# Hymba layer on one core: loads of w_down columns by row block instead of by expert

## Chip, cores and metric

The kernel runs on one core of one Trainium2 chip. The metric is the device time of one execution in microseconds, as the median of several runs.

## What is computed

One layer of a decoder trunk for 256 tokens of width 2048 in float32: a combined projection with a convolution group and an attention group, an output projection, a mixture of experts (32 experts, two for each token), and a gated embedding branch. The change touches the last product of the experts and, through the order of loads, the gate product behind it:

```python
h = h + mixed @ w_out[i]
h = h + hierarchical_moe(rms_norm(h, norm_ffn[i]), ...)
gate = jax.nn.sigmoid(rms_norm(h, norm_ple[i]) @ w_ple_gate[i])
h = h + gate * (p[i] @ w_ple[i])

def expert_block(args):                     # for each expert e
    xb = xt[toks]                           # its tokens
    hidden = jax.nn.silu(xb @ w_gate[e]) * (xb @ w_up[e])
    y = hidden @ w_down[e]                  # w_down[e]: 512 x 2048
    return y * ws[:, None].astype(y.dtype)
```

All weights are float32 and each is read once, some 480 MB in all.

## The kernel before

**Waves.** The 32 experts are worked on in eight waves of four. In a wave each expert has up to 32 tokens, and the four experts share TensorE: expert e of the wave uses the column strip `tile_position=(0, 32 * e)`, so four matmuls of 32 columns run side by side. `gate_up` multiplies the tokens with w_gate and w_up, and its result is turned into `hTw(w)`: for each of four blocks j of 128 rows of w_down, the stationary operand of 32 columns per expert. Each float32 matmul of this kind shows as two records, called passes here.

**w_down.** For a wave, 512 output columns are 16 matmuls: for j in 0..3, for e in 0..3, all accumulating over j in one PSUM tile. For waves 0 to 3 (`NROW` is 4) `down_rows` does all four blocks of 512 columns straight after `gate_up`, from loads of whole rows (`want_rows`). For waves 4 to 7 `down_rows` does the first 1024 columns, from loads of half rows (`want_halves`); in wave 7 it runs all j of the first 512 columns and then all j of the second. The last 1024 columns of waves 4 to 7 come after all waves: `down_wave` runs for w = 4..7 with columns 1024 to 1535 (`TC[2]`) and then for w = 4..7 with columns 1536 to 2047 (`TC[3]`), eight calls in all, from loads that `want_d` lists. Between these calls stand steps of the gate product (`steps(1)`, 12 matmuls at lines 1176 to 1178) and `scatter` (line 1078), which adds a wave's result to the tokens.

**What follows a wave.** `outputs` lets ScalarE write `yh` (line 1071) and VectorE `yl` (line 1072) from the PSUM tile; `scatter` needs both. After the last call come an activation table load (line 1267), a cast and a subtraction of the next gate weight piece (`split`, lines 347 and 348, from a load of w_ple_gate), `add_down` (line 1123), the transposes of the last 512 columns, the last eight gate steps and the output (lines 1306 to 1309).

**Loads.** The order of all loads is a list that `want` fills. `pump` issues them from SyncE's queue (line 76) in this order as long as one of the 26 ring tiles of 1 MB (`NSLOT`) is free; `free(n)` gives back n tiles in program order and calls `pump`. A load whose tile was used before waits on SyncE for the last reader of that tile. Behind the half rows of wave 7 the list holds, in turns, four loads of `want_d` for one wave and, behind six of the eight waves, two loads of w_ple_gate, then two more of w_ple_gate at the very end.

The lines that the prediction follows:

```python
def want_d(w, c0, n):
    for e in range(4 * w, 4 * w + 4):
        want(("d", e, c0), [128, 4, n], w_down[e].rearrange("(j p) n -> p j n", p=128)[:, :, c0:c0 + n])
```

Of the kernel before, what the change touches and what calls it, by code (L numbers as in the profile page):

```python
# [25 lines left out]
NROW = 4  # L26
# [4 lines left out]
def kernel(ctx: ExitStack, tc: tile.TileContext, I, out):  # L31
    nc = tc.nc
    x, p = I["x"][0], I["p"][0, 0]
    w_in, w_out = I["w_in"][0], I["w_out"][0]
    w_gate, w_up, w_down = I["w_gate"][0], I["w_up"][0], I["w_down"][0]
# [18 lines left out]
    def alloc(shape, dt, name):  # L54
        used[0] += 1
        if name != "ld":
            KEEP[0] = max(KEEP[0] - 1, 0)
        assert used[0] <= NSLOT, (name, used, KEEP, nxt, loads[nxt[0]][0])
        return R.tile(shape, dt, name=name, tag="ring")

    loads, nxt, arrived = [], [0], {}

    def want(key, shape, src):
        loads.append((key, shape, src))

    def pump():
        while nxt[0] < len(loads) and used[0] < NSLOT - KEEP[0]:
            key, shape, src = loads[nxt[0]]
            nxt[0] += 1
            t = alloc(shape, F32, "ld") if shape else None  # L70
            i = 0
            for part in src if isinstance(src, list) else [src]:
                if callable(part):
                    part()
                    continue
                nc.sync.dma_start(t[:, i] if isinstance(src, list) else t, part)  # L76
                i += 1
            arrived[key] = t

    def free(n=1):  # L80
        used[0] -= n
        pump()

    def ps():
        return PS.tile([128, 512], F32, name="pst", tag="ps")

    def pa():
        return PA.tile([128, 2, 512], F32, name="pat", tag="pa")
# [47 lines left out]
                         wt[e].rearrange("(p j) f -> p j f", j=16)[:, 4 * j4:4 * j4 + 4, :])  # L136

    def want_d(w, c0, n):
        for e in range(4 * w, 4 * w + 4):
            want(("d", e, c0), [128, 4, n], w_down[e].rearrange("(j p) n -> p j n", p=128)[:, :, c0:c0 + n])  # L140

    def want_rows(w):
        for j in range(4):
# [1 line left out]
                want(("r", e, j), [128, D], w_down[e, 128 * j:128 * j + 128, :])  # L145

    def want_halves(w):
        for jp in range(2):
            for e in range(4 * w, 4 * w + 4):
                want(("r", e, jp), [128, 2, 1024],  # L150
                     w_down[e, 256 * jp:256 * jp + 256, 0:1024].rearrange("(j p) n -> p j n", p=128))

    TC = [(0, 512), (512, 512), (1024, 512), (1536, 512)]
    w_pg_v = w_pg.rearrange("(k p) n -> p k n", p=128)
# [21 lines left out]
    for (ci, w), nxt_ in zip(order, halves_):  # L176
        want_d(w, *TC[ci])
        if nxt_:
            want_pg(nxt_[0], 2 * nxt_[1], 2 * nxt_[1] + 1)
# [839 lines left out]
    def down_rows(w):  # L1019

        hv = hTw(w).rearrange("p (j s) -> p j s", j=4)
        nn = 4 if w < NROW else 2
        pts = [ps() for _ in range(nn)]

        def block(j, n):
            for e in range(4):
                if w < NROW:
                    d = arrived["r", 4 * w + e, j]
                else:
                    d = arrived["r", 4 * w + e, j // 2][:, j % 2]  # L1030
                nc.tensor.matmul(pts[n][32 * e:32 * e + 32, :], hv[:, j, 32 * e:32 * e + 32],  # L1031
                                 d[:, 512 * n:512 * n + 512], start=j == 0, stop=j == 3, tile_position=(0, 32 * e))

        def sums(n, y):
            ns = slice(512 * n, 512 * n + 512)
            po = pa()
            scatter(po, w, y, True, True)
            for tt in range(2):
                if w == 0:
                    if n == 0:  # L1040
                        macc[tt] = alloc([128, D], F32, "macc")
                    nc.vector.tensor_copy(macc[tt][:, ns], po[:, tt])
                else:
                    to = (hmid if w == NW - 1 else macc)[tt][:, ns]
                    nc.vector.tensor_add(to, po[:, tt], to)

        if w == NW - 1:
            for j in range(4):
                block(j, 0)
            y = outputs(pts[0], w)  # L1050
            for j in range(4):
                if j == 2:
                    sums(0, y)
                block(j, 1)
            free(8)
            y = outputs(pts[1], w)
            rows(0)
            sums(1, y)
            return
        for j in range(4):  # L1060
            for n in range(nn):
                block(j, n)
            if w < NROW or j % 2:
                free(4)
        for n in range(nn):
            sums(n, outputs(pts[n], w))

    def outputs(pt, w):

        yh, yl = (w2([128, 512], nm, F32R) for nm in ("yh", "yl"))  # L1070
        nc.scalar.activation(yh, pt, AF.Copy, scale=sw[:, w:w + 1])  # L1071
        nc.vector.scalar_tensor_tensor(yl, pt, sw[:, w:w + 1], yh.bitcast(F32), op0=OP.mult, op1=OP.subtract)  # L1072
        return yh, yl

    def scatter(po, w, y, start, stop):
        for tt in range(2):
            for i in range(2):
                nc.tensor.matmul(po[:, tt], sT(w)[:, 128 * tt:128 * tt + 128], y[i],  # L1078
                                 start=start and i == 0, stop=stop and i == 1)
# [29 lines left out]
    def down_wave(w, c0, cn):  # L1109

        pt = ps()
        hv = hTw(w).rearrange("p (j s) -> p j s", j=4)
        for j in range(4):
            for e in range(4):
                nc.tensor.matmul(pt[32 * e:32 * e + 32, :], hv[:, j, 32 * e:32 * e + 32],  # L1115
                                 arrived["d", 4 * w + e, c0][:, j, :],
                                 start=j == 0, stop=j == 3, tile_position=(0, 32 * e))
        free(4)
        return outputs(pt, w)

    def add_down(po, c0, cn):
# [20 lines left out]
    def rows(ci):  # L1142

        c0, cn = TC[ci]
        kn, k0 = cn // 128, c0 // 128
        hs = hsb[ci % 2]
        src = []
        for tt in range(2):
            src.append(ps().rearrange("p (k t) -> p k t", k=4))
            for kk in range(kn):  # L1150
                nc.tensor.transpose(src[tt][:, kk], acc[tt][:, c0 + 128 * kk:c0 + 128 * kk + 128], ident)
        for tt in range(2):
            tm = w2([128, 4, 128], "tm")
            nc.vector.tensor_tensor(tm, src[tt],
                                    g_ple[:, k0:k0 + kn, None].to_broadcast([128, kn, 128]), op=OP.mult)
            hh = hs[:, :, 128 * tt:128 * tt + 128]
            nc.scalar.copy(hh, tm)
            nc.vector.tensor_sub(hs[:, :, 256 + 128 * tt:384 + 128 * tt], tm, hh.bitcast(F32))
# [88 lines left out]
    for w in range(NROW, NW):  # L1247
        y = down_wave(w, *TC[2])
        steps(1)
        scatter(po, w, y, w == NROW, w == NW - 1)  # L1250
        if w < NW - 1:
            steps(1)
            if w == NROW:
                rows(1)
                squares(1)
            steps(1)
# [185 lines left out]
```

## Time and profile before

| | |
|---|---|
| median of 3 runs | 1362.25 us (1362.24 to 1362.37) |
| profiled execution, its own time | 1362.01 us |
| profiled execution, span of the trace | 1360.3 us |
| TensorE matmuls busy | 1137.8 us, 84% of the span |
| VectorE / ScalarE / GpSimd busy | 410.6 / 265.8 / 122.6 us |
| data moved | 484.29 MB, mean 356 GB/s |
| share of DMA in the chain that ended last | 48% |
| share of TensorE in it | 40% |

The times of the trace count from the start of its span. A busy share is a mean over stages with different limits, so it is read by stretch. Matmuls are pipelined: where one stands still for its data, the records before it are still running, and the idle time shown is shorter than the time lost. A share of DMA above 1 means that packets overlap on the engines.

### The profile page before, as it was taken

How to read it: one execution, taken by the hardware profiler on the slowest of the kernel's cores; microseconds unless marked ns; L12 is line 12 of the kernel's file. 1: busy time of each engine (PE TensorE's matmuls, PEld its weight loads, DVE VectorE, ACT ScalarE, POOL GpSimd, SP SyncE). 2: the span in 40 equal slices, each digit the busy share in tenths (PEclk: the TensorE clock that was granted, in tenths of full speed). 3: DMA queues.
4: the chain of work that ended last, by engine and by line, in shares of the span. 5: the costliest groups of instructions: out<-in, count | busy, mean ns of one | idle time of the engine just before them, and what ended most of it. 6: DMA issues, size and time to landing. Idle time of an engine off the chain costs nothing.

```text
span 1360.3 us, 14996 instructions
## 1 busy us (share of the span) xinstructions
PE 1137.8 (84%) x6171; PEld 633.3 (47%) x6172; DVE 410.6 (30%) x623; ACT 265.8 (20%) x435; POOL 122.6 (9%) x150
## 2 busy tenths in 40 slices
PE   8999899999998787668677775966986876689997
PEld 7888778888663251215125121511531511136655
DVE  6747877655411210201111020110110120124536
ACT  6435455544101000000000000000010000024324
POOL 2214577100000000000000000000000000000000
PEclk9999999999998888889879879998988988889999
DMA  8992245976899999999999999999999999999981
GB/s 261 311 343 80 77 154 175 376 240 221 345 421 420 421 421 421 421 422 420 422 421 421 422 421 422 414 420 421 414 420 421 415 420 422 414 396 394 392 339 63
DMA packets 133141, 484.29 MB, mean 356 GB/s; under 512 B 12020, under 2 KB 49292, under 8 KB 92876
## 3 DMA queue, kind: packets, MB, share of 16 engines
q1 hardware_dynamic: 131916, 480.37, 89.6%
q0 software_dynamic: 864, 2.40, 0.5%
q8 instruction: 50, 0.82, 0.2%
q10 hardware_dynamic: 288, 0.52, 0.2%
q14 instruction: 23, 0.19, 0.0%
HBM read 478.80 MB, written 4.19 MB: 355 GB/s over the span
## 4 chain that ended last, share of the span: by engine, by line
DMA 48%; PE 40%; DVE 5%; ACT 3%; issue 2%; SPq 1%; POOL 1%; ACTq 0%; DVEq 0%; POOLq 0%
DMA ld<-in_w_up_dram 33%; DMA ld<-in_w_down_dram 14%; PE pat L774 7%; PE pst L955 5%; PE pat L971 4%; PE pat L775 3%; PE pat L752 2%; PE pat L754 2%; PE pat L753 2%; PE pst L1115 2%; SPq L76 1%; PE pst L1098 1%; PE pst L1031 1%; DVE wsp L348 1%; PE pat L1078 1%
## 5 line engine op out<-in xcount | busy, mean ns | idle before, releaser
L971 PE MATMUL pat<-ld,xg 128*32 128x512 f32 x2048 | 328.2, 674 | 105.7 <-DMA ld<-in_w_up_dram 60.7
L971 PEld LDWEIGHTS pat<-ld,xg 128*32 128x32 f32 x2048 | 77.1, 121 | 345.9 <-issue 154.6
L774 PE MATMUL pat<-xs,wsp 128*128 128x512 f32 x544 | 197.1, 404 | 0.0
L1031 PE MATMUL pst<-ld,wv 128*32 128x512 f32 x768 | 151.9, 777 | 47.5 <-DMA ld<-in_w_down_dram 42.7
L775 PE MATMUL pat<-xs,wsp 128*128 128x256 f32 x544 | 154.0, 283 | 1.5 <-DVE wsp L348 1.5
L348 DVE TENSOR_TENSOR wsp<-ld,wsp 128x1024 fp32r<-128x1024 f32 x91 | 131.0, 1444 | 74.8 <-ACT wsp L347 74.8
L957 DVE TENSOR_TENSOR xg<-pst,gffn 128x512 f32<-128x512 f32 (+1 forms) x33 | 22.3, 676 | 400.1 <-PE pst L955 400.1
L347 ACT CAST wsp<-ld 128x1024 fp32r<-128x1024 f32 x104 | 107.9, 1048 | 87.2 <-PE pat L754 43.9
L955 PEld LDWEIGHTS pst<-sel,x 128*128 128x128 f32 x512 | 112.7, 311 | 8.4 <-issue 5.0
L774 PEld LDWEIGHTS pat<-xs,wsp 128*128 128x128 f32 x544 | 103.5, 190 | 27.8 <-issue 2.9
L955 PE MATMUL pst<-sel,x 128*128 128x128 f32 x512 | 114.8, 384 | 0.0
L1031 PEld LDWEIGHTS pst<-ld,wv 128*32 128x32 f32 x768 | 33.0, 135 | 160.4 <-DMA ld<-in_w_down_dram 80.8
L1008 ACT ACTIVATE sg<-pat 128x512 f32<-128x512 f32 x8 | 4.8, 597 | 523.3 <-PE pat L971 523.3
L775 PEld LDWEIGHTS pat<-xs,wsp 128*128 128x128 f32 x544 | 104.3, 192 | 2.4 <-DVE wsp L348 2.4
L1072 DVE SCALAR_TENSOR_TENSOR yl<-pst,sw,yh 128x512 fp32r<-128x512 f32 x32 | 23.9, 747 | 229.4 <-ACT yh L1071 229.4
L1071 ACT ACTIVATE yh<-pst,sw 128x512 fp32r<-128x512 f32 x32 | 22.0, 688 | 239.1 <-PE pst L1031 181.1
L948 POOL TENSOR_TENSOR sel<-sel,et 128x128 f32<-128x128 f32 x16 | 6.1, 400 | 643.2 <-DVE sel L946 643.2
L1078 PE MATMUL pat<-yl,wv 128*128 128x512 f32 x64 | 31.6, 493 | 27.4 <-DVE yl L1072 27.3
L752 PE MATMUL pat<-wsp,mx 128*128 128x512 f32 (+1 forms) x128 | 49.8, 389 | 0.1
L753 PE MATMUL pat<-wsp,mx 128*128 128x512 f32 (+1 forms) x128 | 49.0, 383 | 0.0
L754 PE MATMUL pat<-wsp,mx 128*128 128x512 f32 (+1 forms) x128 | 49.0, 383 | 0.0
L348 DVE TENSOR_TENSOR wsq<-ld,wsq 128x1024 fp32r<-128x1024 f32 x32 | 38.6, 1222 | 15.9 <-ACT wsq L347 15.9
(273 smaller groups left out, 1065.1 us busy)
## 6 DMA issues: line engine op xcount, KB each, us to landing
ld<-in_w_gate_dram SPq DMA_DIRECT2D x128, 1024.0 KB, 19.8
ld<-in_w_up_dram SPq DMA_DIRECT2D x128, 1024.0 KB, 11.1
ld<-in_w_down_dram SPq DMA_DIRECT2D x128, 1024.0 KB, 19.8
ld<-in_w_in_dram SPq DMA_DIRECT2D x35, 1024.0 KB, 13.1
ld<-in_w_out_dram SPq DMA_DIRECT2D x16, 1024.0 KB, 8.2
ld<-in_w_ple_gate_dram SPq DMA_DIRECT2D x16, 1024.0 KB, 17.1
spill<-x POOLq DMA_DIRECT2D x8, 256.0 KB, 4.8
ld<-in_w_ple_dram SPq DMA_DIRECT2D x2, 1024.0 KB
```

The source lines that it names most:

```text
L347: copy(t[:, :, 0], src)
L348: eng.tensor_sub(t[:, :, 1], src, t[:, :, 0].bitcast(F32))
L752: nc.tensor.matmul(o, mh, ws[:, kk, 0, cs], start=first, stop=False)
L753: nc.tensor.matmul(o, mh, ws[:, kk, 1, cs], start=False, stop=False)
L754: nc.tensor.matmul(o, ml, ws[:, kk, 0, cs], start=False, stop=last)
L774: nc.tensor.matmul(pt[:, b, :], ws[:, kk, 0, bs], xk, start=first, stop=False)
L775: nc.tensor.matmul(pt[:, b, 0:256], ws[:, kk, 1, bs], xk[:, 0:256], start=False, stop=last)
L955: nc.tensor.matmul(pt[:, 128 * jj:128 * jj + 128], hmid[tt][:, j::16], sel[w][:, tt], start=tt == 0, stop=tt == 1)
L971: nc.tensor.matmul(pt[32 * e:32 * e + 32, n, :], g[:, j, 32 * e:32 * e + 32], wt, start=j == 0, stop=j == 15, tile_position=(0, 32 * e))
L1031: nc.tensor.matmul(pts[n][32 * e:32 * e + 32, :], hv[:, j, 32 * e:32 * e + 32], d[:, 512 * n:512 * n + 512], start=j == 0, stop=j == 3, ti ...
L1078: nc.tensor.matmul(po[:, tt], sT(w)[:, 128 * tt:128 * tt + 128], y[i], start=start and i == 0, stop=stop and i == 1)
L1115: nc.tensor.matmul(pt[32 * e:32 * e + 32, :], hv[:, j, 32 * e:32 * e + 32], arrived["d", 4 * w + e, c0][:, j, :], start=j == 0, stop=j == ...
```

## The change

A load for `down_wave` still holds 512 columns in a tile of 128 partitions x 4 x 512. Before, the 4 are the row blocks j of one expert; after, they are the four experts of the wave, for one row block j. A load of half rows still is 128 x 2 x 1024. Before, the 2 are two neighbouring row blocks of one expert, and the loads of a wave come as experts 0 to 3 for blocks 0 and 1, then for blocks 2 and 3; after, the 2 are two neighbouring experts, for one row block, and the loads come block by block. The matmuls and their order stay. Tiles are given back after each block: one in `down_wave`, two in `down_rows` for half rows (wave 7 still gives back its eight at the end).

```diff
     def want_d(w, c0, n):
-        for e in range(4 * w, 4 * w + 4):
-            want(("d", e, c0), [128, 4, n], w_down[e].rearrange("(j p) n -> p j n", p=128)[:, :, c0:c0 + n])
+        for j in range(4):
+            want(("d", w, j, c0), [128, 4, n],
+                 w_down[4 * w:4 * w + 4, 128 * j:128 * j + 128, c0:c0 + n].rearrange("e p n -> p e n"))
...
     def want_halves(w):
-        for jp in range(2):
-            for e in range(4 * w, 4 * w + 4):
-                want(("r", e, jp), [128, 2, 1024],
-                     w_down[e, 256 * jp:256 * jp + 256, 0:1024].rearrange("(j p) n -> p j n", p=128))
+        for j in range(4):
+            for e in range(4 * w, 4 * w + 4, 2):
+                want(("r", e, j), [128, 2, 1024],
+                     w_down[e:e + 2, 128 * j:128 * j + 128, 0:1024].rearrange("e p n -> p e n"))
...
                 if w < NROW:
                     d = arrived["r", 4 * w + e, j]
                 else:
-                    d = arrived["r", 4 * w + e, j // 2][:, j % 2]
+                    d = arrived["r", 4 * w + e // 2 * 2, j][:, e % 2]
...
         for j in range(4):
             for n in range(nn):
                 block(j, n)
-            if w < NROW or j % 2:
-                free(4)
+            free(4 if w < NROW else 2)
...
         for j in range(4):
             for e in range(4):
                 nc.tensor.matmul(pt[32 * e:32 * e + 32, :], hv[:, j, 32 * e:32 * e + 32],
-                                 arrived["d", 4 * w + e, c0][:, j, :],
+                                 arrived["d", w, j, c0][:, e, :],
                                  start=j == 0, stop=j == 3, tile_position=(0, 32 * e))
-        free(4)
+            free()
         return outputs(pt, w)
```

The order of instructions on every engine stays; what moves is which of them wait for a load. On TensorE, the last call of `down_wave` (wave 7, columns 1536 on) before; `ld` is a load's tile, `wv` holds hTw, and DMAHW5, 6, 7 and 0 are the semaphores of its four loads in the order of issue:

```order
L1178 MATMUL pst<-wsq_5924,hs 128x512
L1115 MATMUL pst<-ld,wv 32x512 [waits DMAHW5_49]
L1115 MATMUL pst<-ld,wv 32x512 [waits DMAHW6_49]
L1115 MATMUL pst<-ld,wv 32x512 [waits DMAHW7_49]
L1115 MATMUL pst<-ld,wv 32x512 [waits DMAHW0_49]
L1115 MATMUL pst<-ld,wv 32x512 x12
```

and the same call after:

```order
L1178 MATMUL pst<-wsq_5924,hs 128x512
L1115 MATMUL pst<-ld,wv 32x512 [waits DMAHW5_49]
L1115 MATMUL pst<-ld,wv 32x512 x3
L1115 MATMUL pst<-ld,wv 32x512 [waits DMAHW6_49]
L1115 MATMUL pst<-ld,wv 32x512 x3
L1115 MATMUL pst<-ld,wv 32x512 [waits DMAHW7_49]
L1115 MATMUL pst<-ld,wv 32x512 x3
L1115 MATMUL pst<-ld,wv 32x512 [waits DMAHW0_49]
L1115 MATMUL pst<-ld,wv 32x512 x3
```

The wait for the fourth load has moved from the fourth of the 16 matmuls to the thirteenth.

On TensorE, the half rows of wave 7 in `down_rows` before, from the third load on (DMAHW1 to DMAHW6 are loads three to eight; the rows behind the last x4 belong to the second 512 columns):

```order
L1031 MATMUL pst<-ld,wv 32x512 [waits DMAHW1_49]
L1031 MATMUL pst<-ld,wv 32x512 [waits DMAHW2_49]
L1031 MATMUL pst<-ld,wv 32x512 x4
L1031 MATMUL pst<-ld,wv 32x512 [waits DMAHW3_49]
L1031 MATMUL pst<-ld,wv 32x512 [waits DMAHW4_49]
L1031 MATMUL pst<-ld,wv 32x512 [waits DMAHW5_49]
L1031 MATMUL pst<-ld,wv 32x512 [waits DMAHW6_49]
L1031 MATMUL pst<-ld,wv 32x512 x4
L1031 MATMUL pst<-ld,wv 32x512 [waits PE_49]
L1031 MATMUL pst<-ld,wv 32x512 x7
```

and after, from the fourth load on, where the line has the number 1032:

```order
L1032 MATMUL pst<-ld,wv 32x512 [waits DMAHW2_49]
L1032 MATMUL pst<-ld,wv 32x512
L1032 MATMUL pst<-ld,wv 32x512 [waits DMAHW3_49]
L1032 MATMUL pst<-ld,wv 32x512
L1032 MATMUL pst<-ld,wv 32x512 [waits DMAHW4_49]
L1032 MATMUL pst<-ld,wv 32x512
L1032 MATMUL pst<-ld,wv 32x512 [waits DMAHW5_49]
L1032 MATMUL pst<-ld,wv 32x512
L1032 MATMUL pst<-ld,wv 32x512 [waits DMAHW6_49]
L1032 MATMUL pst<-ld,wv 32x512
L1032 MATMUL pst<-ld,wv 32x512 [waits PE_49]
L1032 MATMUL pst<-ld,wv 32x512 x7
```

The wait for the eighth load has moved from the twelfth of the 16 matmuls of the first 512 columns to the fifteenth, and every second matmul waits for a load.

## Rows read from the trace of the kernel before

**Rows 1.** The page's slices: busy tenths in 40 slices of 34 us.

```profile
PE   8999899999998787668677775966986876689997
...
DMA  8992245976899999999999999999999999999981
```

**Rows 2.** Stretches: engines' busy us (instructions), TensorE's granted clock, DMA share, GB/s.

```profile
core 0: us, PE busy (x) PEld busy (x) DVE busy (x) ACT busy (x) POOL busy (x), PEclk, DMA share, GB/s
266.00:278.00 12.00, 12.00 (x54) 9.94 (x54) 6.93 (x8) 4.41 (x5) 0.00 (x0) 1.00 1.04 384
540.00:850.00 310.00, 225.70 (x1182) 79.63 (x1178) 37.30 (x73) 10.62 (x16) 2.27 (x6) 0.87 1.01 421
872.00:884.00 12.00, 8.94 (x72) 2.72 (x68) 1.38 (x2) 1.18 (x2) 0.00 (x0) 0.87 1.02 409
1266.00:1274.00 8.00, 8.00 (x41) 6.67 (x40) 6.48 (x10) 1.84 (x3) 0.00 (x0) 1.00 1.05 387
1294.00:1304.00 10.00, 10.00 (x63) 6.04 (x59) 4.31 (x5) 2.68 (x3) 0.00 (x0) 1.00 1.04 385
...
1202.00:1207.00 5.00, 4.80 (x26) 1.14 (x26) 0.71 (x1) 0.69 (x1) 0.00 (x0) 0.69 1.05 389
...
1211.00:1318.00 107.00, 105.86 (x584) 67.05 (x582) 51.27 (x60) 38.37 (x56) 0.00 (x0) 1.00 1.04 393
```

**Rows 3.** TensorE's timeline, wave 7 half rows: start, us, line, xrecords, [idle before <-releaser].

```profile
1199.64 1.05 PE L1031 MATMUL pst<-ld,wv 128*32 128x512 f32 x2 [1.52 <-DMA ld<-in_w_down_dram]
1202.20 5.05 PE L1031 MATMUL pst<-ld,wv 128*32 128x512 f32 x26 [1.51 <-DMA ld<-in_w_down_dram]
```

**Rows 4.** Groups by line, TensorE, 1211 to 1318 us: busy us, mean ns | idle before.

```profile
L1115 PE MATMUL pst<-ld,wv 128*32 128x512 f32 x256 | 31.1, 595 | 0.5 <-DMA ld<-in_w_down_dram 0.5
```

**Rows 5.** TensorE's timeline, four of the eight w_down waves.

```profile
1259.31 1.06 PE L1115 MATMUL pst<-ld,wv 128*32 128x512 f32 x6
1260.88 3.62 PE L1115 MATMUL pst<-ld,wv 128*32 128x512 f32 x26 [0.51 <-DMA ld<-in_w_down_dram]
...
1293.01 3.64 PE L1115 MATMUL pst<-ld,wv 128*32 128x512 f32 x32
...
1303.21 4.03 PE L1115 MATMUL pst<-ld,wv 128*32 128x512 f32 x32
...
1313.80 4.22 PE L1115 MATMUL pst<-ld,wv 128*32 128x512 f32 x32
```

**Rows 6.** The chain that ended last, from 1318 us: start, us, what.

```profile
1318.05 0.03 ACT yh L1071
...
1318.76 1.28 ACT L1267
...
1320.26 0.95 ACT wsq L347
...
1323.65 0.61 DVE x L1123
...
1354.47 0.69 DVE so L1308
```

**Rows 7.** SyncE's loads issued from 254 to 278 us: ns, first and last start.

```profile
L76 SPq DMA_DIRECT2D ld<-in_w_gate_dram x3: 368/1687/2863, 254.4 to 272.0; - x3
L76 SPq DMA_DIRECT2D ld<-in_w_up_dram x3: 367/368/1221, 258.7 to 277.4; - x3
...
DMA to landing us min/median/max: 11.1/11.1/11.1
```

**Rows 8.** SyncE's timeline: the last w_down load, the next of w_ple_gate.

```profile
1300.21 2.60 SPq L76 DMA_DIRECT2D ld<-in_w_down_dram  x1
1302.90 2.50 SPq L76 DMA_DIRECT2D ld<-in_w_ple_gate_dram  x1
```

**Rows 9.** Time from issue to landing of the loads issued from 1180 to 1320 us.

```profile
DMA to landing us min/median/max: 14.1/14.4/18.9
```

**Rows 10.** What SyncE waited for from 1211 to 1318 us: total, times, longest.

```profile
SPq L76 <- PE pat L1178: 15.3, 7, 5.3
```

## Prediction

> **What bounds the kernel now.** I read four views in this order: the page's slices, the rates of a few stretches, TensorE's waits and timeline in the last 120 us, and the chain of waits from 1300 us on. In the slices [rows 1] the reader is to see that the DMA row stands at 9 from about 350 us until close to 1320 us, while TensorE's row is below that in the middle and at 9 only towards the end. So one stretch is bound by the load stream, and a last one may be bound by either.
>
> The rates say how firmly the stream is bound [rows 2]. Loads of 8 KB pieces (gate and up) move at 421 GB/s, half rows (4 KB pieces) at 409, loads of 512 columns (2 KB pieces) at 385 to 387. A stretch of one kind has one rate, whatever TensorE does in it: at 540 to 850 us TensorE is busy for 226 of 310 us and the rate is 421. The stream sets its own pace, and TensorE follows it up to the half rows of wave 7. Work that TensorE finishes earlier in waves 4 to 6 is therefore given back: the next thing it waits for is a later load of the same stream.
>
> From 1202 us on this turns. TensorE's last wait for half rows ends at 1202.20 [rows 3], and in the 107 us from 1211 to 1318 it is busy for 105.86, at a granted clock of 1.00 (2.4 GHz), with 0.5 us of idle before the w_down matmuls as the largest of its idle items [rows 2, 4]. Both are close to full there: the stream moves 393 GB/s, what two thirds at 386 and one third at 409 give.
>
> The idle time hides most of what the loads cost. The 16 matmuls of one w_down wave (32 passes, two for each) take 3.64 us when nothing is late (the wave at 1293.01 [rows 5]). The wave at 1259.31 ran six passes, waited, and needed 3.62 us more from 1260.88 on, so it ended 1.55 us late; the idle shown is 0.51, because the other three experts' column strips still ran a little while. The reason is in the order of the matmuls: block 0 reads all four experts, hence all four loads, and the strip of the fourth expert has all its eight passes ahead when its load lands. Two more waves show it without any idle row: 4.03 us at 1303.21 (0.39 late) and 4.22 us at 1313.80 (0.58 late).
>
> After 1318 us the load stream is over and the end hangs on ScalarE and VectorE: the chain goes from yh at 1318.05 over a table load, a cast and VectorE's steps on to the last store [rows 6]. Everything there starts from the end of the last w_down wave.
>
> **The change part by part.** Bytes, loads, their order by size, matmuls and their order are the same. Loads, 64 in number: each still fills 1 MB with pieces as long as before (4 KB for 32 loads, 2 KB for 32). What differs in a load is the distance between the pieces of one partition, 1 MB before and 4 MB after. The trace has loads of that kind: the first gate and up loads take four experts each, 2 KB pieces 4 MB apart. They are issued from some 255 us on and land 11.1 us later [rows 7]; the stretch in which the first four of them land, 266 to 278 us, runs at 384 GB/s against 385 and 387 for w_down with 1 MB [rows 2]. At 409 and 386 GB/s the 64 loads take 82 + 87 = 169 us, so the 0.3 to 0.8% between those rows bound the cost between nothing and 1.3 us. I take nothing, since 384 is nearest to the 385 of pure w_down, and other shapes differ far more. For half rows no row has 4 MB; I use the same bounds.
>
> A rule speaks against the change here. The Trainium skill, page "DMA: Bandwidth & Descriptors", section "Latency and other measured facts", says that copies whose rows lie a large power of two apart slow down, from 207 to 103 GB/s as the pitch from partition to partition goes from 512 KiB to 4 MiB. By that, were it to hold for the pitch inside a partition, the 64 loads would take about twice their time. The gate loads above do not show it.
>
> Wave 7 of the half rows. Before, after the last landing (1202.20) the fourth strip has block 2, block 3 and the first two blocks of the second column half left: eight passes, done at 1202.20 + 5.05 = 1207.25 [rows 3]. After, the last load holds block 3 of two experts, and these strips have two passes less. A pass costs (3.64 - 0.59) / 7 = 0.44 us at full clock (0.59 is one pass from start to end, 595 ns on the mean [rows 4]), and the clock in this stretch is 0.69 [rows 2], part of it at 1.2 GHz. So 0.9 to 1.7 us are saved; I take 1.0.
>
> The eight w_down waves. After, block j needs load j only. Where TensorE is late, all loads are there and nothing changes; where the stream is late, only the last block, two passes, follows the last landing instead of eight. The three late waves give back 1.55 + 0.39 + 0.58 = 2.5 us. With the half rows this makes 3.5 us that TensorE could gain.
>
> The stream caps this. The last w_down load arrives when the fourth strip starts, at 1313.80 + 0.58 = 1314.4; issued at 1300.21 and with the 14.1 to 14.4 us from issue to landing [rows 8, 9] it comes to 1314.3 to 1314.6, so it agrees. From there the wave takes 3.62 us before, and 0.44 + 0.59 = 1.03 after: it ends at 1315.4 instead of 1318.0. That is **2.6 us**, and it does not depend on the half rows: without their gain TensorE has 2.5 of it, with it the cap binds and about a microsecond goes into a new wait ahead of block 3.
>
> Is the whole of it passed on? Next in the chain are yh, the table load and a cast of the first gate weight piece, which then runs at 1320.2 - 2.6 = 1317.6. Its load is issued at 1302.90 [rows 8], 2.7 us behind the last w_down load, one load of 4 KB pieces (2.56 us), so it lands at 1317.0 to 1317.3. It just fits; here 0.3 us of cover is all there is, and each microsecond that the load is later costs a microsecond of the gain.
>
> SyncE: four tiles come free one by one instead of at once, so a load can only be issued sooner. SyncE waits there for TensorE's gate steps 15.3 us in total [rows 10], but the stream is full all the same, so I count nothing. New waits stand on TensorE alone; behind them in its queue is the rest of the same wave.
>
> Sum: 1362.01 us for the profiled execution (span 1360.3), minus 2.6, is 1359.4. The median of the runs is 0.24 above that execution, so I forecast 1359.65 us, 0.19% less. About 0.2% (2.7 us) is what a measurement of this kernel tells from no change; the forecast lies right under it.
>
> **The rivals.** First, longer jumps do slow the loads. The stream is bound from 350 us to the last w_down load, so each per cent on the 64 loads costs 1.7 us on the end. From 1.5% on the gain is gone, from 3.1% on the kernel is slower by over 0.2%. The largest step between two shapes that rows show is 421 to 385, 8.5%: +14.4 - 2.6 = +12, some 1374 us. For it speaks that 4 KB pieces at 4 MB are not in the trace; against it the 384 GB/s of the gate loads. The rule named above is this rival in its strongest form: 169 us more, some 1530 us.
>
> Second, TensorE or the first gate weight piece comes later than I count. If the clock stays at 1.2 GHz for 4 us more behind 1207, TensorE loses 2 us and has 2.5 + 1.0 - 2.0 = 1.5 us; if the piece lands a microsecond later, 1.6 us are left. Both come to about 1360.7. For it: the granted clock is 0.69 between 1202 and 1207. Against it: it is 1.00 from 1211 on, and the work there is the same.
>
> Third, the loads of a wave land together, so that their order inside a wave decides nothing: 1362.2. Against it, the waits of wave 7 end 2.56 us apart (1199.64, 1202.20 [rows 3]).
>
> Fourth, tiles that come free sooner let the stream run ahead and the last load lands up to 1 us sooner: 1358.7. Against it, 393 GB/s is already what the mix allows.
>
> **How the numbers follow.** Forecast 0.66 (1359.1 to 1360.2; 0.28 of it beyond 0.2%, 0.38 within); slowed loads 0.09, of which 0.01 for the strong form; a later start 0.12; no effect 0.05; a faster stream 0.08. Faster by over 0.2%: 0.28 + 0.08 = 0.36. Within 0.2%: 0.38 + 0.12 + 0.05 = 0.55. Slower: 0.09. The range 1358.3 to 1362.3 takes in all but the slowed loads and the edges.
>
> **What would show it.** In the profile after, 2 KB stretches at 385 to 387 GB/s and half rows at 409 show the loads unharmed; a lower rate is the first rival. The last w_down wave should end near 1315.4, with at least twelve of its matmuls begun before its last load lands, and a wait of up to a microsecond ahead of the last four. The last VectorE step should end 2.6 us sooner than 1355.2 [rows 6]. I am wrong if that wave ends at 1318, if the cast behind it waits for its load, or if the span shrinks by what waves 4 to 6 gained as well.

## Result: the changed kernel is 0.8% slower

The kernel after the change takes 1374.45 us (median of 5 runs, 1369.55 to 1375.29), the one before 1362.37 us (5 runs, 1362.24 to 1363.34): a ratio of 1.0081, 95% interval 1.0066 to 1.0095. The forecast was 1359.65 us. The profiled execution took 1374.57 us with a span of 1372.8, which is 12.5 us more than before.

The slices of the page of after, to be held against [rows 1]; the second row is GB/s, whose last six slices read 414 396 394 392 339 63 before:

```profile
PE   8999889999997786778678677877787776698987
...
GB/s 276 319 312 86 69 154 189 386 225 238 349 421 421 421 421 421 421 422 421 422 421 421 421 421 421 407 422 421 408 422 420 412 421 421 409 362 363 369 292 63
```

Up to slice 35 the load stream has almost the old rates. In slices 36 to 38, some 1200 to 1300 us, it moves 362 to 369 GB/s where 392 to 396 were. Stretches of after, with the columns of [rows 2]:

```profile
872.00:884.00 12.00, 8.94 (x68) 2.62 (x64) 1.38 (x2) 1.18 (x2) 0.00 (x0) 0.86 1.01 387
1266.00:1274.00 8.00, 5.12 (x19) 2.88 (x20) 2.22 (x3) 1.62 (x2) 0.00 (x0) 0.79 1.00 336
...
1211.00:1318.00 107.00, 99.54 (x544) 63.16 (x541) 49.87 (x58) 39.04 (x56) 0.00 (x0) 0.98 1.01 363
```

Gate and up loads run at 421 as before (slices). Half rows fall from 409 to 387 GB/s in the short stretch shown (over the longer one from 860 to 890 us the loss is smaller, see below), and the stretch of w_down columns and w_ple_gate falls from 393 to 363, with a DMA share of 1.01 instead of 1.04. TensorE is busy for 99.5 of 107 us instead of 105.9.

TensorE's timeline in after (half rows now on line 1032), to be held against [rows 3, 5]:

```profile
1203.39 4.74 PE L1032 MATMUL pst<-ld,wv 128*32 128x512 f32 x20 [0.63 <-DMA ld<-in_w_down_dram]
...
1268.88 1.93 PE L1115 MATMUL pst<-ld,wv 128*32 128x512 f32 x8 [3.59 <-DMA ld<-in_w_down_dram]
...
1310.22 2.78 PE L1115 MATMUL pst<-ld,wv 128*32 128x512 f32 x24
1314.34 1.07 PE L1115 MATMUL pst<-ld,wv 128*32 128x512 f32 x8 [1.33 <-DMA ld<-in_w_down_dram]
1321.98 2.78 PE L1115 MATMUL pst<-ld,wv 128*32 128x512 f32 x24
1327.59 1.94 PE L1115 MATMUL pst<-ld,wv 128*32 128x512 f32 x8 [2.83 <-DMA ld<-in_w_down_dram]
```

The waits are where the forecast put them: 24 of 32 passes run, then the last block waits, and only eight passes follow the last landing. But that landing is at 1327.59 instead of 1314.4. TensorE's waits and SyncE's, from 1211 to 1331 us, against [rows 4, 10], and two rows of the chain that ended last:

```profile
PE pst L1115 <- DMA ld<-in_w_down_dram: 9.6, 5, 3.6
...
SPq L76 <- PE pst L1115: 23.1, 10, 6.6
...
1309.94 17.60 DMA ld<-in_w_down_dram
1327.59 1.94 PE pst L1115 x8
```

The idle ahead of the w_down matmuls is 9.6 us instead of 0.5, and SyncE, which waited for gate steps before, now waits 23.1 us for w_down matmuls that stand still for late loads. The last steps, against [rows 6]:

```profile
1327.00:1333.00 6.00, 5.41 (x16) 3.05 (x17) 0.99 (x2) 3.11 (x4) 0.00 (x0) 0.50 0.60 244
...
1366.97 0.69 DVE L1308 TENSOR_TENSOR so<-so,x 128x512 f32<-128x512 f32 x1
```

So the 12.5 us are made up like this. The last load lands 13.2 us later (1327.59 - 1314.4). The forecast gain behind a landing is 2.6 us. Behind the 2.83 us in which TensorE stood still, the granted clock is 0.50 (1.2 GHz), so the eight passes take 1.94 instead of 1.03 us (0.9 more). The first gate steps behind them run at that clock too (0.43 us each instead of 0.23), and another 1.0 is lost: from the end of the wave to the start of the last VectorE step it is 37.4 us instead of 36.5. 13.2 - 2.6 + 0.9 + 1.0 = 12.5.

### The profile page after: what moved, and what is told of

Read it like the earlier page. It is cut to its first block, busy times and chain, and to the rows that moved or that the text cites. A ratio compares the mean times of both kernels' runs of the same rounds, so it can differ in the third digit from the quotient of the medians.

```text
span 1372.8 us, 15000 instructions
## 1 busy us (share of the span) xinstructions
PE 1141.8 (83%) x6171; PEld 635.3 (46%) x6172; DVE 409.8 (30%) x623; ACT 265.6 (19%) x435; POOL 122.9 (9%) x150
## 4 chain that ended last, share of the span: by engine, by line
DMA 53%; PE 36%; DVE 5%; ACT 3%; issue 2%; POOL 1%; SPq 0%; ACTq 0%; DVEq 0%; POOLq 0%
DMA ld<-in_w_up_dram 35%; DMA ld<-in_w_down_dram 17%; PE pat L775 6%; PE pst L956 5%; PE pat L972 4%; PE pat L776 3%; PE pat L753 2%; PE pat L755 2%; PE pat L754 2%; PE pst L1032 2%; DMA ld<-in_w_ple_dram 1%; PE pst L1115 1%; DVE wsp L349 1%; PE pst L1176 1%; ACT wsp L348 1%
## 5 line engine op out<-in xcount | busy, mean ns | idle before, releaser
L775 PE MATMUL pat<-xs,wsp 128*128 128x512 f32 x544 | 194.0, 399 | 0.0
## 6 DMA issues: line engine op xcount, KB each, us to landing
ld<-in_w_in_dram SPq DMA_DIRECT2D x35, 1024.0 KB, 12.5
```

The lines of the kernel that those rows point to most:

```text
L775: nc.tensor.matmul(pt[:, b, :], ws[:, kk, 0, bs], xk, start=first, stop=False)
```

## Experiments

### One part at a time

The change to `want_d` and `down_wave` alone:

```diff
-        for e in range(4 * w, 4 * w + 4):
-            want(("d", e, c0), ...)
+        for j in range(4):
+            want(("d", w, j, c0), [128, 4, n],
+                 w_down[4 * w:4 * w + 4, 128 * j:128 * j + 128, c0:c0 + n].rearrange("e p n -> p e n"))
```

> Only the loads of want_d are by row block, with their waits and the release tile by tile; the half rows are as before. Theory D (distance: pieces of a partition 4 MB apart are served slower, wherever such a load stands): the lag of the last w_down load, 13 us in the profile after, comes nearly all from these 32 loads: 1371 to 1375 us. Theory W (waits: the pieces are served as before, but tiles given back one by one and waits spread over a wave make SyncE issue late, 23 us of waiting for L1115 against 3.7 before): also slow, 1371 to 1375. Theory H (the half rows start the lag and the rest follows): 1359.7 to 1362.

Measured: 1370.48 us against 1362.17, ratio 1.0065 (1.0048 to 1.0081). In its trace the last w_down wave (here on line 1116) waits 1.50 us, and its eight passes keep the full clock:

```profile
1324.15 1.06 PE L1116 MATMUL pst<-ld,wv 128*32 128x512 f32 x8 [1.50 <-DMA ld<-in_w_down_dram]
...
1361.68 0.69 DVE L1309 TENSOR_TENSOR so<-so,x 128x512 f32<-128x512 f32 x1
```

The last load is 9.8 us late, and the last VectorE step 7.2 us (1361.68 against 1354.47): 9.8 minus the forecast gain of 2.6, with nothing added for the clock. Half rows block by block alone:

```diff
-        for jp in range(2):
-            for e in range(4 * w, 4 * w + 4):
+        for j in range(4):
+            for e in range(4 * w, 4 * w + 4, 2):
                 want(("r", e, j), ...)       # two experts, block j
```

> Only the half rows are by row block; want_d and down_wave are as before. Theory D: the four groups of half rows lose some 1.2 us together (last half row 1203.39 after against 1202.20 before), and the rest of the stream follows at 2.7 us a load as before: 1361.5 to 1364. Theory W: no loss, 1361 to 1362.5. Theory H: 1370 or more.

Measured: 1363.98 us, ratio 1.001 (1.0001 to 1.002). The half rows' stretch from 860 to 890 us moves 406 GB/s, against 413 before; the one from 1260 to 1310 us, where loads of columns and of w_ple_gate run, keeps 390. Before, and half rows by block:

```profile
860.00:890.00 30.00, 24.56 (x155) 13.45 (x158) 4.12 (x7) 1.18 (x2) 0.00 (x0) 0.94 1.02 413
...
860.00:890.00 30.00, 25.72 (x166) 14.17 (x165) 4.12 (x7) 1.18 (x2) 0.00 (x0) 0.94 1.02 406
```

The column loads carry most of the loss, the half rows some 1.8 us (interval 0.1 to 2.7).

### The loads by block with the old waits

```diff
-        for j in range(4):
+        for k in range(4):
             for e in range(4):
+                j = (k + e) % 4
                 nc.tensor.matmul(..., hv[:, j, ...], arrived["d", w, j, c0][:, e, :],
-                                 start=j == 0, stop=j == 3, ...)
+                                 start=k == 0, stop=k == 3, ...)
         free(4)
```

The first four matmuls need all four loads, as before, and the tiles are given back together.

> The loads of want_d are by row block, but a wave is consumed along diagonals (first block e of expert e, and so on), so that the first four matmuls wait for all four loads as before, and the four tiles are given back together as before; the half rows are as before. Theory D: as slow as the by-block loads alone or slower, since a late load now holds up the whole wave: 1372 to 1378. Theory W: the old waits bring the old time, 1361.5 to 1363.

Measured: 1374.14 us (1368.91 to 1376.23), ratio 1.0072 (1.0047 to 1.0097); 1260 to 1310 us at 363 GB/s. The loss is there without the new waits, so these don't make it. It isn't smaller either; whether the new waits win something back here (1370.48 with them) can't be told, as the ranges overlap.

### Loads alone

SyncE issues 32 loads of one pattern, VectorE copies one column of each of eight tiles when they have landed, and the next pattern begins.

> Leaves out the whole layer and writes zeros; it only streams loads of 1 MB from SyncE over eight tiles, 32 loads to a phase, with a barrier between phases, the six phases twice over: w_down 512 columns by expert (pieces 1 MB apart), by block (4 MB), along diagonals (5 MB), half rows by expert (1 MB), half rows by block (4 MB), and w_gate rows of four experts (4 MB apart, partitions 32 KB apart instead of 8). Theory D: the by-block phases are slower, 355 to 375 GB/s against 386 and 395 to 405 against 409, and the diagonals (not a power of two) may be at 386. Theory W: 385 to 387 in all 512-column phases, 409 in both of half rows, no phase under another.

VectorE's timeline; the number in brackets is what VectorE waited for the last load of the group, so the time of the group. In order: by expert, by block, diagonals (first row of two), half rows by expert, half rows by block, gate weights as in wave 0:

```profile
656.12 0.88 DVE L49 COPY acc<-t 128x1 f32<-128x1 f32 x8 [89.19 <-DMA t<-in_w_down_dram]
752.57 0.67 DVE L49 COPY acc<-t 128x1 f32<-128x1 f32 x6 [95.40 <-DMA t<-in_w_down_dram]
...
841.81 0.88 DVE L49 COPY acc<-t 128x1 f32<-128x1 f32 x8 [87.82 <-DMA t<-in_w_down_dram]
938.38 0.88 DVE L49 COPY acc<-t 128x1 f32<-128x1 f32 x8 [95.52 <-DMA t<-in_w_down_dram]
1034.11 0.88 DVE L49 COPY acc<-t 128x1 f32<-128x1 f32 x8 [94.69 <-DMA t<-in_w_down_dram]
1126.01 0.88 DVE L49 COPY acc<-t 128x1 f32<-128x1 f32 x8 [90.85 <-DMA t<-in_w_gate_dram]
```

By block costs 6.2 us more than by expert with no matmul anywhere. The gate weights, 4 MB apart as well, cost 1.7; half rows by block cost nothing. (Half rows run at 373 to 379 GB/s in the middle of their groups here in either order, not at the kernel's 409, so this stream is a weak test of them.) And diagonals, where expert e contributes block (k+e) modulo 4 so that the pieces lie 5 MB apart, cost nothing. In the middle of its group each pattern of 2 KB pieces moves 385 to 387 GB/s. The by-block group loses its time elsewhere: 6 us close to its end run at 326 GB/s, those of the diagonals at 386:

```profile
120.00:185.00 65.00, 0.00 (x0) 0.00 (x0) 1.00 1.05 387
186.00:192.00 6.00, 0.00 (x0) 0.00 (x0) 1.00 0.87 326
205.00:275.00 70.00, 0.00 (x0) 0.00 (x0) 1.00 1.05 386
276.00:282.00 6.00, 0.00 (x0) 0.00 (x0) 1.00 1.05 386
```

A DMA share that falls while bytes are still missing says that some DMA engines are done and others are behind. The trace shows this directly: besides the views it keeps the times of sixteen landing signals for every DMA, as many as the core has DMA engines. A wait ends with the last of them (in the kernel after, the last signal of the last w_down load is at 1327.55, and TensorE starts at 1327.59). By expert, the sixteen come within 0.4 to 1.2 us, along diagonals within 0.3 to 1.0. By block the time from first to last grows over the first six loads of the group to 4.5 us and stays there, in both rounds.

### Which distances

> Loads alone, in groups of 32 with a barrier behind each; the layer is left out and zeros are written. 2 KB pieces of w_down, four to a partition, 1, 2, 3, 4, 5, 6, 7, 8 and 16 MB apart, then gate weights 4 MB apart with partitions 2 KB apart and with partitions 32 KB apart; all twice. Theory D: 4, 8 and 16 MB (the multiples of 4) take 94 to 97 us for a group, odd distances 87 to 89.5, 2 and 6 in between or like the odd ones; gate weights with partitions 2 KB apart take 94 or more, with 32 KB 90. Rival D2 (four experts in one load): the time grows from 1 to 3 MB on in steps and 5 and 7 are as slow as 4.

The same timeline, w_down pieces 2, 3, 4, 5, 6, 8 and 16 MB apart, first round:

```profile
189.58 0.87 DVE L49 COPY acc<-t 128x1 f32<-128x1 f32 x8 [90.82 <-DMA t<-in_w_down_dram]
280.18 0.26 DVE L49 COPY acc<-t 128x1 f32<-128x1 f32 x2 [89.56 <-DMA t<-in_w_down_dram]
...
377.57 0.88 DVE L49 COPY acc<-t 128x1 f32<-128x1 f32 x8 [95.94 <-DMA t<-in_w_down_dram]
467.73 0.88 DVE L49 COPY acc<-t 128x1 f32<-128x1 f32 x8 [89.11 <-DMA t<-in_w_down_dram]
559.49 0.87 DVE L49 COPY acc<-t 128x1 f32<-128x1 f32 x8 [90.72 <-DMA t<-in_w_down_dram]
...
746.63 0.67 DVE L49 COPY acc<-t 128x1 f32<-128x1 f32 x6 [95.95 <-DMA t<-in_w_down_dram]
...
844.62 0.88 DVE L49 COPY acc<-t 128x1 f32<-128x1 f32 x8 [96.59 <-DMA t<-in_w_down_dram]
```

4, 8 and 16 MB cost 95.9 to 96.6 us, 1, 3, 5 and 7 MB 89.0 to 89.6, 2 and 6 MB 90.7 to 90.8; the second round agrees within 0.5. It is neither a matter of long distances nor of four experts in one load, but of multiples of 4 MB. The landing signals split the same way: 4.6 to 5.8 us from first to last with 4, 8 and 16 MB, at most 1.9 with all others. Gate weights 4 MB apart take 89.7 to 90.2 with partitions 2 KB apart and 90.6 with 32 KB.

### The diagonals in the kernel

```diff
+        blocks = w_down[4 * w:4 * w + 4].rearrange("e (j p) n -> p (e j) n", p=128)[:, :, c0:c0 + n]
+        for k in range(4):                  # piece e is block (k + e) % 4 of expert e
+            m = 4 - k
+            nxt_t = [(slice(0, m), blocks[:, k:k + 5 * m - 4:5])]
+            if k:
+                nxt_t.append((slice(m, 4), blocks[:, 4 * m:4 * m + 5 * k - 4:5]))
+            want(("d", w, k, c0), [128, 4, n], nxt_t)
...
-        for j in range(4):
+        for k in range(4):
             for e in range(4):
+                j = (k + e) % 4
```

with `free()` after each k, as in the change.

> Half rows as before. Each load of the last 1024 columns holds one row block of each expert, but a different block per expert (expert e has block (k+e) modulo 4), so its pieces lie 5 MB apart instead of 4; the matmuls run in that order, so that as with the changed loads only the last four wait for the last load, and the tiles come free one by one. Loads whose diagonal wraps round are issued as two DMAs. Theory D (4 MB between the pieces of a partition lets some DMA engines fall behind): the diagonals ended without a tail in the streams alone, so the forecast gain of the new waits comes: 1358.5 to 1361, the last w_down load lands at 1314 to 1316, stretches of 2 KB pieces stay at 385 GB/s or more. Rival D2 (any distance over 1 MB, or four experts in one load, does it): 1368 to 1374. Rival D3 (it is the order of the waits and the tiles given back one by one): 1368 to 1374 too, but then loads by block with the old waits would have been quick, which they were not.

Measured: 1361.78 us (11 runs) against 1363.91 (21 runs), ratio 0.9989 (0.998 to 0.9998). The control, by block (4 MB) but cut into as many DMAs as the diagonals:

```diff
-            nxt_t = [(slice(0, m), blocks[:, k:k + 5 * m - 4:5])]
+            nxt_t = [(slice(0, m), blocks[:, k:k + 4 * m - 3:4])]
...
-                j = (k + e) % 4
+                j = k
```

> The control for the diagonals: loads of one row block of four experts (4 MB between the pieces), each issued in two DMAs as the diagonals are (4, then 3 and 1, 2 and 2, 1 and 3 pieces). Half rows as before. If the distance alone makes the loss: 1368 to 1372, as with one DMA for each load (1370.5). If cutting loads in two is what helps the diagonals: the time of the diagonals, 1358.5 to 1361.

Measured: 1371.61 us, ratio 1.0069 (1.0042 to 1.0096). More DMAs don't help; the distance does. Then diagonals for the half rows too (pieces 5 MB apart in three of four loads, 1 MB in the fourth):

```diff
+        for k in range(4):
+            for e in range(4 * w, 4 * w + 4, 2):
+                b, d = 4 * e + k, 5 if k < 3 else 1
+                want(("r", e, k), [128, 2, 1024], blocks[:, b:b + d + 1:d])
```

> Diagonals for the last 1024 columns and for the half rows too (two experts per load, neighbouring blocks: 5 MB apart for three of four loads, 1 MB for the fourth). Theory D: half rows at 409 GB/s again, last one landed by 1202.5; 1358 to 1361, not slower than diagonals for the last columns alone. Theory H (half rows block by block start a lag of engines whatever their distance): 1 to 3 us more than the diagonals for the last columns alone.

Measured: 1361.93 us, ratio 0.9989 (0.998 to 0.9998), and on another chip once more:

> Diagonals for the last 1024 columns and for the half rows, once more against the kernel before: 0.997 to 0.9995 of its time, if the forecast mechanism of the waits holds (1359.65 of 1362.25 is 0.998); 1.000 if the gain of the first comparison was chance.

1361.78 us against 1363.21, ratio 0.999 (0.9981 to 0.9999). This version has the waits of the change without its distances, and its median is 0.1% under that of the kernel before on both chips, with intervals that end just below 1. Its trace is close to what the forecast had described. Windows, the last half rows, the last w_down wave, the cast behind it and the last VectorE step, from the first chip (the quickest of the eleven runs there), and as the last row the last wave on the second chip:

```profile
860.00:890.00 30.00, 25.42 (x168) 13.57 (x171) 4.12 (x7) 1.18 (x2) 0.00 (x0) 0.94 1.02 413
...
1211.00:1318.00 107.00, 106.66 (x591) 68.36 (x592) 51.14 (x60) 40.97 (x59) 0.00 (x0) 1.00 1.04 393
...
1202.07 4.22 PE L1043 MATMUL pst<-ld,wv 128*32 128x512 f32 x20 [1.51 <-DMA ld<-in_w_down_dram]
...
1311.06 4.23 PE L1127 MATMUL pst<-ld,wv 128*32 128x512 f32 x32
...
1317.46 1.03 ACT L357 CAST wsq<-ld 128x1024 fp32r<-128x1024 f32 x1
...
1351.77 0.69 DVE L1320 TENSOR_TENSOR so<-so,x 128x512 f32<-128x512 f32 x1
...
1311.92 3.94 PE L1127 MATMUL pst<-ld,wv 128*32 128x512 f32 x32
```

The span does not keep all of it. From the end of the last VectorE step to the end of the span 6.1 us pass instead of 5.1, so it is 1.7 us shorter (1358.6 against 1360.3) where that step is 2.7 us sooner. The other three runs with loads cut into two DMAs show 6.1 to 6.2 us there too, the control by block among them, and none of the kernels without such cuts more than 5.5. So the cutting seems to cost about a microsecond at the end; where, stays open.

### What in the addresses, and what of it in a mix

> Loads alone, in groups of 32 loads of four 2 KB pieces to a partition, a barrier behind each group, everything twice; the layer is left out and zeros are written. First part, pieces 4 MB apart in all cases, partitions different: w_down as the change loads it (partitions 8 KB apart), w_down with partitions 32 KB apart, gate weights with partitions 8 KB apart, w_down with 4 MB and one row of 8 KB between the pieces, w_down with 4 MB and one piece of 2 KB. Theory A (addresses alone: 4 MB between pieces and 8 KB between partitions fall together): 96, 90, 96, 89 to 90, 89 to 90 us. Rival B (it is the array w_down, or quarter rows, at any multiple of 4 MB): 96, 96, 90, and the last two near 96. Second part, tiles given back by VectorE one by one, as a kernel does: by expert (1 MB) and by block (4 MB) with 16, 8 and 5 tiles in flight. Theory C (some DMA engines fall behind, and with few tiles the others then stand still): by expert 89 to 90 with 16 and 8 and a little more with 5; by block 96 with 16 and 97 to 100 with 5. Rival E (the loss is the end of a group only): by block minus by expert stays 6 to 7 us for all three.

Here a group's time is the step from VectorE's memsets behind one group to those behind the next. The first part, in us (the first group of all has no step ahead of it):

| distance of pieces | of partitions | first round | second |
|---|---|---|---|
| w_down, 4 MB | 8 KB | | 96.7 |
| w_down, 4 MB | 32 KB | 90.9 | 90.0 |
| gate weights, 4 MB | 8 KB | 104.3 | 102.8 |
| w_down, 4 MB + 8 KB | 8 KB | 96.6 | 96.6 |
| w_down, 4 MB + 2 KB | 8 KB | 89.4 | 90.4 |

So it is not the array: gate weights lose more. It needs both strides (partitions 8 KB apart and a multiple of 4 MB between the pieces), and a shift of one piece undoes it while a shift of one row doesn't. With theory A the shift by a row should have helped, so that part of it fell. By block minus by expert is 97.2 - 90.2, 97.0 - 90.4 and 96.9 - 90.7 us with 16, 8 and 5 tiles: 6 to 7 us whatever the number of tiles. Theory C fell. The number is the one of rival E, but not the place, the end of a group. The landings of the by-block group with eight tiles (VectorE's copy of each load as it lands) tell where the 7 us are:

```profile
760.83 0.36 DVE L54 MEMSET t<- 128x1 f32 x16
769.80 0.15 DVE L48 COPY acc<-t 128x1 f32<-128x1 f32 x1 [8.61 <-DMA t<-in_w_down_dram]
774.20 0.15 DVE L48 COPY acc<-t 128x1 f32<-128x1 f32 x1 [4.24 <-DMA t<-in_w_down_dram]
777.10 0.15 DVE L48 COPY acc<-t 128x1 f32<-128x1 f32 x1 [2.75 <-DMA t<-in_w_down_dram]
780.39 0.15 DVE L48 COPY acc<-t 128x1 f32<-128x1 f32 x1 [3.14 <-DMA t<-in_w_down_dram]
...
795.21 0.15 DVE L48 COPY acc<-t 128x1 f32<-128x1 f32 x1 [2.57 <-DMA t<-in_w_down_dram]
```

The first seven loads land late, one after the other; from then on they come every 2.71 us, as by expert. A lag grows at the start, and stays. A stretch of one kind pays it once. But the column loads of the kernel came 12 us late, not 7, and the kernel doesn't have stretches of one kind there: behind six of the eight waves come two loads of w_ple_gate. Hence the last stream, which mixes them.

> Loads alone, with the other loads of the kernel between them, VectorE giving the tiles back one by one, 16 tiles; the layer is left out and zeros are written. Eight groups of four loads of w_down columns and two of w_ple_gate: by expert, by block, along diagonals; then four groups of eight half rows and eight gate loads: by expert, by block; everything twice. In the streams of one kind the loss by block stood at the start of a stretch only, some 7 us whatever the number of tiles. Theory F (each change to the other kind of load and back lets the lag grow anew): by block minus by expert is 10 to 20 us for the column loads, as the kernel's last w_down load was 13.2 us late, and 1 to 4 us for the half rows; diagonals within 1 us of by expert. Theory G (one start, then a steady lag): 6 to 8 us for the column loads, within 1 us for the half rows; the rest of the kernel's 13 us then comes from TensorE's waits and its lower clock.

By block 147.0 us, by expert 131.1, diagonals 131.2 (second round; 147.7 and 131.4 in the first for by block and diagonals); half rows between gate loads 175.2 and 176.7 by expert, 175.9 and 175.2 by block. Landings by block in the second round, from a pair of w_ple_gate loads to the next, and the rates in the middle of by expert, by block and diagonals:

```profile
925.52 0.15 DVE L52 COPY acc<-t 128x1 f32<-128x1 f32 x1 [2.41 <-DMA t<-in_w_ple_gate_dram]
928.21 0.15 DVE L52 COPY acc<-t 128x1 f32<-128x1 f32 x1 [2.54 <-DMA t<-in_w_down_dram]
...
933.40 0.15 DVE L52 COPY acc<-t 128x1 f32<-128x1 f32 x1 [2.38 <-DMA t<-in_w_down_dram]
937.82 0.15 DVE L52 COPY acc<-t 128x1 f32<-128x1 f32 x1 [4.27 <-DMA t<-in_w_down_dram]
...
800.00:890.00 90.00, 5.15 (x34) 0.00 (x0) 1.00 1.04 393
930.00:1040.00 110.00, 5.99 (x39) 0.00 (x0) 1.00 1.01 366
1080.00:1170.00 90.00, 5.22 (x34) 0.00 (x0) 1.00 1.05 394
```

Mixed, the loss comes back in each group: the fourth load lands 4.42 us behind the third, where 2.6 to 2.7 is normal. Of the 15.9 us, 9.2 belong to the first group, and the other seven take 17.02 us each (925.52 to 1044.66, by 7) instead of 16.07. The rates, 393 and 366 GB/s at a DMA share of 1.04 and 1.01, are those of the two kernels (393 and 363, 1.04 and 1.01).

The landing signals of the two kernels show the same step by step. Before, loads land 2.5 to 2.7 us apart from the last half row to the last w_down load. After, the fourth load of a wave comes 4.2 to 5.3 us behind the third, in seven of the eight waves, and all others 2.5 to 2.8. Each time the span from a load's first signal to its last grows by 1.2 to 2.2 us, and shrinks again in the loads that follow. In the kernel before it stays at 6.2 to 6.3 us in this stretch: a lag that stays costs nothing there, one that grows delays all later loads. Theory F holds for the column loads. For the half rows it fails: their 1.8 us in the kernel don't show in a stream.

## Why the prediction was wrong

**What bounds the kernel: right.** The stream sets the pace until its last load, and the end follows from there by a fixed chain. This is why the late landing was passed on whole: 112.2 us lay between the last half row and the last w_down load before, 124.2 after.

**The cost of the loads: the step that failed.** The prediction said "I take nothing, since 384 is nearest to the 385 of pure w_down", with 0 to 1.3 us as bounds. It measured some 12 us for the column loads (last landing 13.2 us late, 1.2 of which stood already at the last half row: 1203.39 against 1202.20, though one run with the old half rows has 1203.91 there), and 9.8 us in the run that changes them alone. The row it rested on has 4 MB between the pieces, but its partitions lie 32 KB apart, where those of w_down lie 8 KB apart. Those were taken for "loads of that kind" because one stride, the one the change alters, agreed. With 8 KB between partitions the same gate weights take 102.8 us instead of 90.6. The second error is smaller: a rate over 12 us of one kind doesn't show a cost that lies in where loads land. The same stretch, which the change doesn't touch, reads 377 GB/s in after and 386 with diagonals in the column loads, so 384 could not have borne the fine bounds.

**The rule of the Trainium skill** (page "DMA: Bandwidth & Descriptors", section "Latency and other measured facts") was closer than the row. Its direction agrees with the streams: 4 MB cost 96.7 us. Its remark that a few KB of padding bring the rate back agrees in part: 2 KB do (89.4 to 90.4 us), 8 KB, the distance between the partitions, don't (96.6). Its size doesn't carry over: it halves the rate for the pitch between partitions, and here, for the distance inside a partition, a group of one kind lost 7% and the mixed one 12%. The prediction set the rule aside because the gate loads "do not show it", with a chance of 0.09 for the rival; given a row that agreed in one stride of two, that was too little.

**The first rival: right in kind, and near in time (1374) by luck, for its price was another.** It took 8.5% on all 64 loads. In truth it was 8% on the stretch of column loads and little on the half rows, and two more microseconds came from the half clock behind TensorE's waits, which no term of the sum had.

**Wave 7 of the half rows: the mechanism right.** In the first trace with both diagonals it ends at 1202.07 + 4.22 = 1206.29 instead of 1207.25: 0.96 us, 1.0 was forecast, though 0.13 of it is an earlier landing. In the second trace 4.60 us pass behind the landing instead of 5.05, so only 0.45 us are saved there. In after the later landing eats it: 1203.39 + 4.74 = 1208.13.

**The waves, the cap and the tail: right, once the loads are unharmed.** Forecast were the end of the last wave at 1315.4, the cast behind it at 1317.6 and the last VectorE step 2.6 us sooner. With both diagonals they are 1315.29, 1317.46 and 2.70 us sooner (1351.77 against 1354.47), and in the second trace 1315.86, 1318.03 and 2.12 us. The medians gained 2.0 and 1.4 us on their chips, and the intervals (0.2 to 2.7 us, 0.1 to 2.6) just hold 2.6; about a microsecond of it goes at the end of the span, as shown above. Of the forecast wait ahead of block 3 there is no idle row in that wave, but 4.23 and 3.94 us instead of 3.64 show that it was still 0.6 and 0.3 late.

**SyncE: wrong in after.** The prediction's "so a load can only be issued sooner" holds only while the matmuls don't stand still: SyncE waited 3.7 us for them in the whole execution before, and 23.1 us in the stretch shown after. The run with the old waits is as slow, so this follows from the late loads and doesn't cause them.

## What to carry to other kernels

A row of the trace prices a new access pattern only if all its strides agree, not just the one that the change alters; where no row has them all, a stream of the loads alone costs one short run, and it has to contain the mix of the kernel, since a pattern can cost less in a stretch of its own (7 us here, against 16 in the mix). If a regrouping of loads puts the pieces of one load a multiple of 4 MB apart, as here with partitions 8 KB apart, rotate the blocks (piece e takes block (k+e) modulo 4): the waits stay the same and the distance becomes 5 MB, at the price of loads cut in two. Behind a bound stream, a late landing can cost more than its delay: 1.9 us more here, in the run in which TensorE's clock had fallen by then, and nothing more in the run in which it had not.

## What the runs showed of the hardware

Loads of 128 x 4 pieces of 2 KB, partitions 8 KB apart: 32 of them take 89.0 to 89.6 us with 1, 3, 5 or 7 MB between the pieces, 90.7 to 90.8 with 2 or 6, 95.9 to 96.6 with 4, 8 or 16. This fits one count: how many of the four pieces of a load lie at the same place when addresses are taken modulo 4 MB (one, two and four). If pieces of neighbouring partitions count too, 4 MB + 2 KB counts as one, and 4 MB + 8 KB as four. The count is argued, not shown, and it holds at most for partitions 8 KB apart: pieces 4 MB apart count as four with any partitions, but cost little with partitions 2 KB apart (gate weights, 89.7 to 90.2) or 32 KB apart (w_down 90.0 to 90.9, gate weights 90.6). What the memory does there stays open.

In a stretch of one kind the loss is not a lower rate but a lag: the rate in the middle stays at 385 to 387 GB/s, while the sixteen landing signals of a load come within 4.5 us instead of about 1.0, and the load is there only with the last. Mixed with w_ple_gate loads, where the lag grows again with nearly every group of four, the rate falls as well (366 against 393 GB/s in the stream, 363 against 393 in the kernel). Why it grows with the fourth load of a group stays open. So does why half rows 4 MB apart lose 1.8 us in the kernel (406 GB/s in both kernels that load them so, 413 in all others) and nothing in two streams.
